# Later gate sums and a later recurrence in the second block's mixer: one core of a Trainium2

## The chip, the cores and the metric

One Trainium2 chip, of which one core is used. The time is the device time of one launch in microseconds (us), the median of three runs. A profiled execution of the same kernel gives the trace that is read below.

## What is computed

The reference is a block with retention, dilated attention and a memory cross-attention, followed by a second block of two layers. Each layer of the second block is a feed-forward network, a mixer, and another feed-forward network; the change touches the mixer alone. It has three branches over 512 positions, whose outputs are normalised one by one, joined, scaled, and projected:

```python
proj = h @ w_in
(lru_x, lru_g, sb_q, sb_k, sb_v, fx_q, fx_k, fx_v, fx_f) = jnp.split(proj, SPLIT_POINTS, axis=-1)
u = _causal_depthwise_conv(lru_x, conv_w, conv_b)
y_lru = _rg_lru(u, w_rgate, b_rgate, w_igate, b_igate, lru_lambda) * jax.nn.gelu(lru_g)
y_sb = _stick_breaking_attention(...)            # four heads, softplus and a running sum per row
log_f = jax.nn.log_sigmoid(fx_f + b_fgate)       # forget gates: their running sum is a bias of the scores
y_fox = _forgetting_attention(fq, fk, ..., log_f)
y = jnp.concatenate([_rms(y_lru), _rms(y_sb), _rms(y_fox)], axis=-1) * g_mix_out
return y @ w_out
```

## The kernel before, in words

All large products run on TensorE (PE) as three products of rounded parts (`mm3`, lines 346 to 348): a weight of 128x1024 is loaded by a DMA on SyncE's queue (SP), rounded by ScalarE (ACT) to `wh`, and the rest `wl` is taken by VectorE (DVE) or GpSimd (POOL). There are three buffers for raw weights and six for each rounded part, so weights come some steps ahead of use.

The order of TensorE's work is written out by a small planner, the class `Flow`: a main generator issues the dense products, and streams (generators that were spawned) issue the attention tiles, norms and the recurrence. Each `yield` tells the planner a cost of TensorE in its own clock, and `Wait(us)` tells it that a stream may not go on before so much planned time. A stream that is due always goes before the next `mm3` of the main generator. TensorE then runs in exactly that order, whatever the real times are. The other engines are ordered at build time by a scheduler that follows dependencies and the order in which the program traced the instructions; each engine then runs its own list in order.

`mixer2(l, ...)` runs once per layer, at about 1279 to 1545 us (layer 0) and 2303 to 2570 us (layer 1) of the span. Its stages, as the main generator goes:

- The last dense product gives the queries and keys of the stick-breaking attention and `fT`, the forget gates' raw values (line 1347).
- A token product (`dense_tok`, tile `mmt`) gives the values `v`, and another one the queries and keys of the forgetting attention. Beside them run `gates()` and four tiles `stick(t)`, t = 3, 2, 1, 0 (512 to 128 columns). A stick tile issues scores, then softplus, a scan and exponentials on ACT, DVE and POOL, waits until `v[t]` has been issued, turns the weights (tile `tp`) and multiplies them with `v` (tile `SO`). Tile t-1 begins when tile t has its softplus behind it by the planner's clock.
- `gates()` was spawned with 1.0 us of delay. It turns `fT` (tile `f`, line 1395), issues the log-sigmoid as some twenty small operations of DVE (`neg_log_sigmoid`, tiles `lp_p` and `ls_r`), waits `gate_f` = 6.0 planned us, asks for the running sums on TensorE (tile `cs`, line 1409), copies them to `NF`, and spreads them over the partitions in four tiles `fb` (line 1418), which the forgetting tiles need.
- The last dense product of eight chunks of eight `mm3` (24 matmuls each) gives the inputs of the recurrence: chunks 0 to 3 the convolution's inputs `LX`, 4 to 7 the gates `LG`. Beside it run the forgetting tiles `fox(t)`, t = 3 to 0, each closed by `finish(o, t, 2)`: squares on ACT (`fsq`), an inverse root of ten small DVE operations (`rs_m` to `rs_y`), the scaled tile `fy`, a planned wait of 4.91 us, and a turn on TensorE (`tp`<-`fy`).
- Also beside it runs the recurrence `lru`. It polls every 0.5 planned us until `opened["last"]` is set, which `fox(0)` did when the scores of its last head were issued. It then loads two gate weights `bd` (256 KB each) by SP, and issues for each of four parts two gate products (tile `lg`, line 1287), their `Tanh` (kept behind the last `Exp` of `fox(0)` on ACT by `issue_after`), and then exponentials, squares on POOL, square roots, products on POOL and scans on DVE. The gelu, the product, the squares and their sum on POOL (`acc`) need `LG` of chunk 7 for the last part.
- When all attention tiles are turned, a product of four weights with the attention outputs follows (`slab4`, tile `sl`, 96 matmuls). The recurrence's own output goes through a second product (tile `slh`), which begins with the column sums of `acc` (tile `ms`, line 464) and their inverse root (tile `bc`).

Of the kernel before, what the change touches and what calls it, by code (L numbers as in the profile page):

```python
# [13 lines left out]
AF = mybir.ActivationFunctionType  # L14
# [171 lines left out]
def _pe(n, passes=4):  # L186

    return passes * max(n, 64) / 2400.0
# [5 lines left out]
         post1=4.2, dil_tail=1.5, dil_end=5.0, dil_turn=2.3, rsqrt=3.51, norm=0.6, post=0.38,  # L194
         apart=8.0, squares=4.73, rope=10.0, rope_k=6.24, ret=4.0, ret_e=2.0, ret_gn=8.0, aq=4.0,
         ak=4.0, dil=2.0, mem=8.0, dil_1=0.11, dil_2=0.5, mem_e=6.32, mem_p=2.24, mem_q=1.5,
         lru_tanh=2.88, lru_sum=25.0, lru_end=2.52, fqk=8.0, gate_f=6.0, gate_s=0.6, finish=4.91,
         fox_1=0.9, fox_2=0.41, stick_2=0.8, stick_h=2.0, stick_o=0.0, stick_l=4.0, stick_m=1.0,
         stick=1.81, first0=10.5, first1=15.9)

# [82 lines left out]
class Core:  # L283
# [985 lines left out]
    def lru(self, l, LX, LG, HL, opened):  # L1269


        nc, I, flow = self.nc, self.I, self.flow
        while "last" not in opened:
            yield Wait(0.5)
        bd = [self.act("bd") for _ in range(2)]
        for q in range(2):
            nc.sync.dma_start(bd[q], I["m_bd"][l][:, q * 512:q * 512 + 512])
        a4, hb = self.a4[l], self.hb[l]
        U, R, G = [], [], []
        for m in range(4):  # L1280
            while len(LX) <= m:
                yield Wait(0.5)
            u = LX[m]
            r, g = self.act("lr"), self.act("li")
            for q, o in enumerate((r, g)):
                ps = self.ps("x", "lg")
                nc.tensor.matmul(ps, bd[q][:, m * 128:m * 128 + 128], u,
                                 start=True, stop=True)

                with self.tc.issue_after(opened["last"]):  # L1290
                    nc.scalar.activation(o, ps, AF.Tanh, scale=0.5,
                                         bias=hb[:, q * 4 + m:q * 4 + m + 1])
                yield _pe(512)
            nc.vector.scalar_tensor_tensor(u, g, 1.0, u, op0=OP.add, op1=OP.mult)

            nc.scalar.activation(g, r, AF.Tanh, scale=a4[:, m:m + 1], bias=a4[:, m:m + 1])
            U.append(u), R.append(r), G.append(g)
        bd.clear()
        for m in range(4):
            c = a4[:, 4 + m:5 + m]  # L1300
            nc.scalar.activation(R[m], R[m], AF.Exp, scale=c, bias=c)
        for m in range(4):
            u, a, g = U[m], R[m], G[m]

            q = self.rot("a2")
            nc.gpsimd.tensor_tensor(q, a, a, op=OP.mult)
            nc.vector.scalar_tensor_tensor(g, q, 1.0, g, op0=OP.add, op1=OP.mult)
        for m in range(4):
            u, a, g = U[m], R[m], G[m]
            nc.scalar.activation(g, g, AF.Sqrt, scale=0.25)  # L1310
            nc.gpsimd.tensor_tensor(u, u, g, op=OP.mult)

            nc.vector.tensor_tensor_scan(g, a, u, 0.0, op0=OP.mult, op1=OP.add)
        while len(LG) < 4:
            yield Wait(0.5)
        sums = []
        for m in range(4):
            nc.scalar.activation(LG[m], LG[m], AF.Gelu_apprx_tanh)
            nc.vector.tensor_tensor(U[m], G[m], LG[m], op=OP.mult)
            self.square_sum(sums, U[m], self.rot)  # L1320
        HL += [(self.act("lh", F32R), self.act("ll", F32R)) for _ in range(4)]

        def norm(hf):
            sl, out = slice(hf * 256, hf * 256 + 256), []
            yield from self.spread([sums[0][:, sl]], 2, 1.0 / 512, out)
            for m in range(4):
                t = self.half("ln")
                nc.vector.scalar_tensor_tensor(t, U[m][:, sl], self.vec(f"g_mix{l}", m), out[0],
                                               op0=OP.mult, op1=OP.mult)
                hi, lo = HL[m][0][:, sl], HL[m][1][:, sl]  # L1330
                nc.scalar.activation(hi, t, AF.Copy)
                nc.vector.tensor_tensor(lo, t, hi.bitcast(F32), op=OP.subtract)
        yield Wait(T["lru_sum"])
        yield from norm(0)
        opened["half"] = flow.t
        yield from norm(1)

    def mixer2(self, l, H, H2):
# [53 lines left out]
        def gates():  # L1392
# [22 lines left out]
            for h in range(4):  # L1415
# [6 lines left out]
                nc.scalar.activation(o, ps, AF.Copy)  # L1422
                FB.append(o)
                yield 4 * _pe(128)
        gated = flow.spawn(gates(), 1.0)

        YT = {}

# [28 lines left out]
        def finish(o, t, y0):  # L1457
# [3 lines left out]
            rs = self.rsqrt(ss, 1, 1.0 / 256, RMS_EPS)  # L1461
            y = self.half("fy")
            nc.vector.tensor_scalar(y, o, rs, None, op0=OP.mult)
            yield Wait(T["finish"])
            ps = self.flip([y[:, p * 128:p * 128 + 128] for p in range(2)])
            sl = slice(t * 128, t * 128 + 128)
# [7 lines left out]
        def fox(t):  # L1474
# [10 lines left out]
            def score(h):  # L1485
                if h % 2 == 0:
# [6 lines left out]
                c = slice(h, h + 1)  # L1493
                nc.vector.tensor_tensor(b[:, c], nf[:, c], m[:, c], op=OP.subtract)
                nc.vector.tensor_tensor(b[:, c], b[:, c], nf[:, c], op=OP.subtract)
                last = nc.scalar.activation(e[:, :n], e[:, :n], AF.Exp, bias=b[:, c],
                                            accum_out=lsum[:, c])
                if (t, h) == (0, 3):
                    opened["last"] = last.ins
                return 0.0 if h % 2 else _pe(n) + 0.2  # L1500

            def second(h):
# [57 lines left out]
        opened = {}  # L1560
# [128 lines left out]
```

## Time and profile before

| | |
|---|---|
| median of 3 runs | 2929.01 us (2927.82 to 2929.83) |
| profiled execution, device time | 2929.86 us |
| its span, first to last instruction | 2928.1 us |
| TensorE busy | 2783.2 us of the span, mean granted clock 0.974 |
| VectorE, ScalarE, GpSimd busy | 1540.9, 1033.7, 382.2 us |

The views are read in this order: the busy share of each engine, TensorE's waits by what ended them, the timelines around the two longest kinds of wait, and the busy times and granted clock of the stretches there. Times in timelines are us from the span's start; a number in square brackets is the idle time of that engine just before, and behind it stands what ended it.

### The profile page before, as it was taken

What the parts mean: (1) busy time and instruction counts of PE and PEld (TensorE: products, weight loads), DVE (VectorE), ACT (ScalarE), POOL (GpSimd) and SP (SyncE); (2) the same over time, 40 slices, a digit from 0 to 9 for tenths busy, and PEclk for the clock granted to TensorE, in tenths of its full rate; (3) what the DMA queues carried; (4) which work ended last, traced back from release to release, by engine and by line L of the source; (5) the groups of instructions that cost most, each with busy time, mean ns of one, the idle gap of its engine ahead of it and who ended that gap; (6) DMA issues with size and microseconds to landing.
All of it is one profiled execution on the core that took longest, in us unless ns stands there. A gap on an engine that the chain in (4) does not pass through costs nothing.

```text
span 2928.1 us, 36992 instructions
## 1 busy us (share of the span) xinstructions
PE 2783.2 (95%) x14492; PEld 2360.2 (81%) x14492; DVE 1540.9 (53%) x2973; ACT 1033.7 (35%) x1739; POOL 382.2 (13%) x376
## 2 busy tenths in 40 slices
PE   8999998999989999979889999999999898899999
PEld 7888878888878888877678888888888775788888
DVE  6465656645455444457666454464334576643333
ACT  4355443323233222345534222342223455342221
POOL 3010304101041000131221000110001312210000
PEclk9999999999989999989989999999999899899999
DMA  4322332645524555311115555354322121232322
GB/s 162 119 75 88 93 94 65 184 159 173 161 86 137 158 173 158 113 53 65 51 59 165 158 173 158 115 166 129 101 94 92 53 65 44 59 100 87 107 87 72
DMA packets 94607, 326.07 MB, mean 111 GB/s; under 512 B 11232, under 2 KB 15584, under 8 KB 94432
## 3 DMA queue, kind: packets, MB, share of 16 engines
q1 hardware_dynamic: 94288, 323.53, 35.4%
q8 instruction: 114, 1.87, 0.3%
q14 instruction: 61, 0.50, 0.1%
q10 hardware_dynamic: 144, 0.18, 0.0%
HBM read 321.37 MB, written 2.10 MB: 110 GB/s over the span
## 4 chain that ended last, share of the span: by engine, by line
PE 84%; DVE 10%; ACT 3%; POOL 2%; issue 1%; DMA 1%; POOLq 0%; ACTq 0%; DVEq 0%
PE mm L346 15%; PE mm L348 15%; PE mm L347 15%; PE dn L348 6%; PE dn L346 6%; PE dn L347 6%; PE mmt L346 2%; PE mmt L347 2%; PE mmt L348 2%; PE slh L347 2%; PE slh L346 2%; PE slh L348 2%; PE tp L684 1%; DVE wl L340 1%; PE sl L347 1%
## 5 line engine op out<-in xcount | busy, mean ns | idle before, releaser
L338 ACT ACTIVATE wh<-wr 128x1024 fp32r<-128x1024 f32 x456 | 481.9, 1059 | 1266.0 <-PE mm L347 504.4
L346 PE MATMUL mm<-hh,wh 128*128 128x512 f32 (+1 forms) x2344 | 862.1, 368 | 4.8 <-ACT hh L527 1.9
L347 PE MATMUL mm<-hl,wh 128*128 128x512 f32 (+1 forms) x2344 | 855.0, 365 | 2.5 <-DVE hl L500 2.4
L348 PE MATMUL mm<-hh,wl 128*128 128x512 f32 (+1 forms) x2344 | 854.3, 364 | 3.0 <-DVE wl L340 3.0
L340 DVE TENSOR_TENSOR wl<-wr,wh 128x1024 fp32r<-128x1024 f32 x440 | 542.6, 1236 | 326.4 <-ACT wh L338 324.9
L346 PEld LDWEIGHTS mm<-hh,wh 128*128 128x128 f32 x2344 | 450.1, 192 | 73.5 <-ACT hh L527 2.2
L348 PEld LDWEIGHTS mm<-hh,wl 128*128 128x128 f32 x2344 | 449.3, 192 | 71.3 <-DVE wl L340 3.6
L347 PEld LDWEIGHTS mm<-hl,wh 128*128 128x128 f32 x2344 | 449.9, 192 | 69.8 <-DVE hl L500 3.2
L795 DVE CUSTOM_DVE_ANT_0 ada<-ada,c 128x1024 f32<-128x1024 f32 x144 | 179.1, 1244 | 317.8 <-DMA ada<-in_w_ada_dram 317.8
L348 PE MATMUL dn<-uh,wl 128*128 128x512 f32 x720 | 280.5, 390 | 0.0
L347 PE MATMUL dn<-ul,wh 128*128 128x512 f32 x720 | 280.5, 390 | 0.0
L346 PE MATMUL dn<-uh,wh 128*128 128x512 f32 x720 | 280.5, 390 | 0.0
L490 POOL TENSOR_TENSOR acc<-sq,sq 128x256 f32<-128x256 f32 (+1 forms) x34 | 38.5, 1133 | 1330.7 <-ACT sq L487 1330.7
L633 DVE TENSOR_TENSOR sg<-mm,sg 128x512 f32<-128x512 f32 x110 | 75.8, 690 | 183.5 <-PE mm L348 179.2
L347 PEld LDWEIGHTS dn<-ul,wh 128*128 128x128 f32 x720 | 135.2, 188 | 28.0
L348 PEld LDWEIGHTS dn<-uh,wl 128*128 128x128 f32 x720 | 135.2, 188 | 28.0
L346 PEld LDWEIGHTS dn<-uh,wh 128*128 128x128 f32 x720 | 135.2, 188 | 27.9
L346 PE MATMUL mmt<-wh,hh 128*128 128x512 f32 x352 | 145.4, 413 | 10.5 <-ACT wh L338 8.0
L347 PE MATMUL mmt<-wl,hh 128*128 128x512 f32 x352 | 140.1, 398 | 0.5 <-DVE wl L340 0.5
L348 PE MATMUL mmt<-wh,hl 128*128 128x512 f32 x352 | 139.8, 397 | 0.0
L490 POOL TENSOR_TENSOR acc<-acc,sq 128x256 f32<-128x256 f32 (+1 forms) x140 | 122.3, 874 | 83.4 <-ACT sq L487 45.0
L669 DVE SCALAR_TENSOR_TENSOR X<-dn,gate,X 128x512 f32<-128x512 f32 x64 | 48.0, 750 | 153.7 <-PE dn L348 153.7
(324 smaller groups left out, 3627.6 us busy)
## 6 DMA issues: line engine op xcount, KB each, us to landing
wr<-in_f_gu_dram SPq DMA_DIRECT2D x176, 512.0 KB, 3.5
ada<-in_w_ada_dram SPq DMA_DIRECT2D x144, 512.0 KB, 4.2
wr<-in_f_dn_dram SPq DMA_DIRECT2D x88, 512.0 KB, 3.5
wr<-in_w_gu_dram SPq DMA_DIRECT2D x44, 512.0 KB, 3.6
wr<-in_w_in_dram SPq DMA_DIRECT2D x28, 512.0 KB, 3.6
wr<-in_m_t_dram SPq DMA_DIRECT2D x24, 512.0 KB, 3.5
wr<-in_w_dn_dram SPq DMA_DIRECT2D x22, 512.0 KB, 3.7
wr<-in_m_v_dram SPq DMA_DIRECT2D x16, 512.0 KB, 3.6
```

Of the source, the lines that this page charges most:

```text
L338: nc.scalar.activation(hi, raw, AF.Copy)
L340: (e or nc.vector).tensor_tensor(lo, raw, hi.bitcast(F32), op=OP.subtract)
L346: mm(ps, ah, bh, start=start, stop=False)
L347: mm(ps, ah, bl, start=False, stop=False)
L348: mm(ps, al, bh, start=False, stop=stop)
L490: nc.gpsimd.tensor_tensor(acc, accs.pop(), sq, op=OP.add)
L633: nc.vector.tensor_tensor(t, ps, t, op=OP.mult)
L669: self.nc.vector.scalar_tensor_tensor(self.X[m], ps, gate(m), self.X[m], op0=OP.mult, op1=OP.add)
L684: self.nc.tensor.transpose(ps[:, j * 128:j * 128 + 128], b, self.ident)
L795: nc.vector.tensor_tensor_reduce(out=w, in0=w, in1=c, scale=1.0, scalar=0.0, op0=OP.mult, op1=OP.add, accum_out=ml[:, i:i + 1])
```

## The change

The wait of `gates()` between the log-sigmoid and the sums grows from 6 to 24 planned us and the stream starts 4.0 instead of 1.0 us after its spawn. `opened["last"]` is now set by `finish` of the last forgetting tile, behind the tracing of its norm; the recurrence polls every 0.3 instead of 0.5 us. The order constraint of `Tanh` behind the last `Exp` goes. After each gate product the stream waits 0.3 planned us, so that one `mm3` of the main generator comes between two products.

```diff
-         lru_tanh=2.88, lru_sum=25.0, lru_end=2.52, fqk=8.0, gate_f=6.0, gate_s=0.6, finish=4.91,
+         lru_tanh=2.88, lru_sum=25.0, lru_end=2.52, fqk=8.0, gate_f=24.0, gate_s=0.6, finish=4.91,
...
         while "last" not in opened:
-            yield Wait(0.5)
+            yield Wait(0.3)
...
-                with self.tc.issue_after(opened["last"]):
-                    nc.scalar.activation(o, ps, AF.Tanh, scale=0.5,
-                                         bias=hb[:, q * 4 + m:q * 4 + m + 1])
+                nc.scalar.activation(o, ps, AF.Tanh, scale=0.5,
+                                     bias=hb[:, q * 4 + m:q * 4 + m + 1])
                 yield _pe(512)
+                yield Wait(0.3)
...
-        gated = flow.spawn(gates(), 1.0)
+        gated = flow.spawn(gates(), 4.0)
...
             nc.vector.tensor_scalar(y, o, rs, None, op0=OP.mult)
+            if (t, y0) == (0, 2):
+
+                opened["last"] = True
             yield Wait(T["finish"])
...
-                last = nc.scalar.activation(e[:, :n], e[:, :n], AF.Exp, bias=b[:, c],
-                                            accum_out=lsum[:, c])
-                if (t, h) == (0, 3):
-                    opened["last"] = last.ins
+                nc.scalar.activation(e[:, :n], e[:, :n], AF.Exp, bias=b[:, c],
+                                     accum_out=lsum[:, c])
```

## Rows read from the trace of the kernel before

**Rows 1.** Part 1 of the page: engines, busy us, share, instructions.
```profile
PE 2783.2 (95%) x14492; PEld 2360.2 (81%) x14492; DVE 1540.9 (53%) x2973; ACT 1033.7 (35%) x1739; POOL 382.2 (13%) x376
```

**Rows 2.** Waits of PE, whole span: engine, line, waited for; us, times, longest.
```profile
PE tp L684 <- DVE fy L1463: 36.4, 4, 16.7
...
PE cs L1409 <- DVE ls_r L1246: 23.7, 2, 12.7
...
PE f L1395 <- ACT fT L1347: 2.9, 2, 1.5
```

**Rows 3.** Timeline (start, us, engine, line, tiles), forget gates of layer 0.
```profile
1302.37 0.18 DVE L1246 TENSOR_TENSOR ls_r<-ls_r,lp_p 128x16 f32<-128x16 f32 x1
...
1302.70 0.56 PE L1409 MATMUL cs<-ls_r,tri 128*128 128x4 f32 x2 [12.74 <-DVE ls_r L1246]
...
1308.38 4.73 PE L1418 MATMUL fb<-ident,NF 128*128 128x128 f32 x32
```

**Rows 4.** Stretches: length, PE, PEld, DVE, ACT, POOL busy, granted clock, DMA, GB/s.
```profile
1289.00:1303.00 14.00, 1.26 (x7) 0.79 (x5) 13.38 (x23) 6.39 (x12) 6.49 (x4) 0.66 0.02 6
1303.00:1308.00 5.00, 5.00 (x23) 4.81 (x23) 0.17 (x1) 0.00 (x0) 0.00 (x0) 0.50 0.00 0
```

**Rows 5.** The same columns, the stretch of the stick tiles behind the sums.
```profile
1303.00:1345.00 42.00, 40.00 (x234) 33.76 (x233) 17.38 (x30) 17.66 (x34) 5.72 (x4) 0.91 0.15 51
```

**Rows 6.** Timeline, stick tile t = 2 of layer 0, and the turns that use it.
```profile
1315.15 0.92 PE L1437 MATMUL S<-sqk,sqk 64*128 64x384 f32 x4
...
1323.82 0.53 ACT L1541 ACTIVATE z<-z 128x384 f32<-128x384 f32 x1 [1.39 <-POOL z L1540]
...
1330.84 0.53 ACT L1541 ACTIVATE z<-z 128x384 f32<-128x384 f32 x1 [1.43 <-POOL z L1540]
...
1332.19 1.69 PE L684 MATMUL tp<-ident,z 128*128 128x128 f32 x14
```

**Rows 7.** Timeline, last two forgetting tiles and gate products; last row is layer 1.
```profile
1439.03 0.40 ACT L1460 ACTIVATE fsq<-fo 128x256 f32<-128x256 f32 x1
...
1440.35 1.13 PE L1287 MATMUL lg<-lx,bd 128*128 128x512 f32 x2
...
1444.44 0.35 DVE L1463 TENSOR_SCALAR fy<-fo,rs_y 128x256 f32<-128x256 f32 x1
...
1446.50 4.51 PE L1287 MATMUL lg<-lx,bd 128*128 128x512 f32 x10
...
1460.27 0.40 ACT L1460 ACTIVATE fsq<-fo 128x256 f32<-128x256 f32 x1
...
1471.83 1.43 DVE L1463 TENSOR_SCALAR fy<-fo,rs_y 128x256 f32<-128x256 f32 x1
...
1473.41 0.66 PE L684 MATMUL tp<-ident,fy 128*128 128x128 f32 x2 [16.73 <-DVE fy L1463]
...
2496.30 0.66 PE L684 MATMUL tp<-ident,fy 128*128 128x128 f32 x2 [16.41 <-DVE fy L1463]
```

**Rows 8.** Stretches (columns of rows 4): cold restart behind the turn, and the attention product.
```profile
1473.00:1478.00 5.00, 4.59 (x13) 3.71 (x14) 2.10 (x4) 0.73 (x2) 0.12 (x1) 0.53 0.31 105
...
1482.00:1502.00 20.00, 20.00 (x89) 16.54 (x89) 10.80 (x13) 4.53 (x6) 1.30 (x1) 1.00 0.30 91
```

**Rows 9.** Timeline, end of the recurrence: its sums on POOL and their use.
```profile
1471.85 1.26 POOL L490 TENSOR_TENSOR acc<-acc,sq 128x512 f32<-128x512 f32 x1
...
1484.84 1.30 POOL L490 TENSOR_TENSOR acc<-acc,sq 128x512 f32<-128x512 f32 x1 [11.72 <-issue]
...
1502.91 0.50 PE L464 MATMUL ms<-ones,acc 128*128 128x1 f32 x4
```

**Rows 10.** Timeline of SP's queue: the gate weights, and the weight loads behind them.
```profile
1430.27 0.90 SPq L1277 DMA_DIRECT2D bd<-in_m_bd_dram  x2
1443.48 31.27 SPq L336 DMA_DIRECT2D wr<-in_m_o_dram  x2
```

**Rows 11.** Stretch (columns of rows 4): forgetting tiles between chunks of the dense product.
```profile
1380.00:1425.00 45.00, 42.60 (x250) 32.78 (x251) 32.12 (x97) 15.63 (x37) 5.83 (x3) 1.00 0.20 59
```

## Prediction

> **What bounds the kernel now.** I read the page first: TensorE is busy for 95% of the span, no other engine for much over half [rows 1]. So a gain can only come from the time in which TensorE stands still or runs at its lower clock, and that is read from its waits. Three of them are in the second block's mixer, once for each layer [rows 2]: turns of `fy` (36.4 us, nearly all of it in two long waits), the sums `cs` behind the log-sigmoid (23.7 us in two), and the turn of `fT` (2.9 us in two). The timelines then say why.
>
> The sums: TensorE comes to `cs` with nothing left to do before it and waits 12.74 us for `ls_r` [rows 3]. In that stretch VectorE is busy for 13.38 of 14 us [rows 4]: the twenty small operations of the log-sigmoid go between the wide ones of stick tile 3. The order asks for the sums too early; other products (`mmt`) stand behind them in TensorE's list and could have run.
>
> The turn of `fy`: the norm of the last forgetting tile begins with its squares on ScalarE at 1460.27, with no idle time of ScalarE ahead of it, 9.3 us after the last gate product ended (1446.50 plus 4.51): its list held the recurrence's functions first. The scaling on VectorE follows at 1471.83, behind the scans, and TensorE waits 16.73 us in layer 0 and 16.41 us in layer 1 [rows 7]. The tile before, whose norm had no recurrence ahead of it, needed 5.8 us from its squares to its `fy` (1439.03 to 1444.79) [rows 7]. Behind each long wait TensorE goes on at its lower level of 1.2 GHz: granted 0.50 and 0.53 in the two stretches that follow [rows 4, 8], against 1.00 in the next product [rows 8].
>
> **Part by part: the sums.** `fT`'s turn moves behind the scores of stick tile 3, by when `fT` is long written: the 2.9 us go, and nothing waits for `f` but the log-sigmoid. The sums move 24 planned us behind that. The first token product is 32 `mm3` of 0.64 planned us, so with the scores of two tiles (2 x 1.05 and 2 x 0.84) it ends at about 24.5 planned us, and the sums stand at about 28.2, among the turns of stick tiles 3 and 2. That is some 20 us of TensorE's work later than now, against a wait of 12.7, so the wait goes: 12.7 and 11.0 us (23.7 less 12.7). The forgetting tiles, which use `fb`, begin only behind the second token product, so nobody misses it. With the wait the restart at 1.2 GHz goes. A stretch of 5 us at 0.50 [rows 4] holds at most 2.5 us of that; with what follows I bound it by 0 and 4 and take 2 per layer, near the row.
>
> What is late next is VectorE. It has the same work, and TensorE is now ahead of it. The turns of stick tiles 3 and 2 stand at 1332.19 [rows 6]. Take off the 12.74, the 1.4 of `fT`, and the sums with `fb`, which now come later (1302.70 to 1313.1 [rows 3] less one `mm3`, 9.1 us), and some 1.5 of clock: they would come at about 1307.5. VectorE is full until 1302.4. Tile 2 needed 9.2 us from its scores to its second head's weights (1315.15 to 1324.35) and 16.2 us to its fourth [rows 6]; if it only gets VectorE at 1302.4, the second head is there at 1311.6, 4 us late. With about 1 us for a copy of `v` or `NF` in ScalarE's or VectorE's list I take 5 us per layer of new waits. Bounds: 0 (tile 2's copies and softplus fit between) and all of 12.7 (VectorE stays the end of the chain). Against the upper one speaks the stretch behind, where VectorE is busy for 17.38 of 42 us [rows 5]: it can catch up. Layer 0: 1.4 + 12.7 + 2 - 5 = 11.1; layer 1: 1.5 + 11.0 + 2 - 5 = 9.5. Together 20.6 us.
>
> **The recurrence.** It now starts when the norm of the last tile has been traced, so squares, root and `fy` stand ahead of it in all lists, and the removed constraint on `Tanh` costs nothing: the products it reads come behind the last tile on TensorE anyway. The two `bd` loads go 10 us later in the program. Now they are issued at 1430.27, ten us before the first product [rows 7, 10]. If SP takes them behind the load at 1443.48 [rows 10], they still land about when the first product stands (1448); behind the second load of that row they would hold TensorE for some us. I take 0, bounds 0 and 8.
>
> TensorE's work is only reordered. At 1440.35 two of eight chunks (16 `mm3`) are left. About seven fill the waits of the last tile where gate products stand now, and the rest alternate with the eight products, which cost 0.90 us each now (five in 4.51 us [rows 7]). The turn of `fy` stands 4.91 planned us behind the norm's tracing, which itself comes 1.09 planned us behind the last product with `v`; that is 6 us and more against the 5.8 measured for the tile before [rows 7], so I leave 0.5 us, bounds 0 and 3. The waits of 16.73 and 16.41 us go. The restart goes too: 13 matmuls took 5 us, and at the rate of the product (89 in 20 us, 0.225 each) they take 2.9 [rows 8]: 2.1 us per layer. Changing between gate products and `mm3` eight times may cost 0.1 us each, 1 us in all with the other engine-side gaps, bounds 0 and 2.
>
> Late next is the recurrence itself. From the last gate product's end (1451.0) to the sum of its third part (1473.1) it took 22.1 us; the fourth sum waited for chunk 7 and adds its own 1.3 us [rows 7, 9], so 23.4 us. In the new order the last product and the last chunk end together, and then the attention product covers 96 x 0.225 = 21.6 us until `ms` asks for the sum (today it asks 16.8 us after it: 1486.14 to 1502.91 [rows 9]). So 2 us of wait per layer; bounds 0 (the first three parts run ahead in the spaced products) and 12 (VectorE's 10.80 us of evacuations and weight parts in 20 us of that product [rows 8] stand ahead of the scans). Per layer: 0.5 + 1 + 2 = 3.5 us of new cost. Sum: 16.73 + 16.41 + 2 x 2.1 - 2 x 3.5 = 30.3 us.
>
> Both parts: 50.9 us. The profiled execution took 2929.86 us, its span 2928.1; minus 50.9 is 2879.0. It lies 0.85 above the median of the runs, so **2878 us**.
>
> **Rivals.** (A) *The stick tiles take the place of the sums' wait*: VectorE's list, not the order, is the end, and only `fT`'s 2.9 us stay of the first part: 2929 - 30.3 - 2.9 = 2896. For it: 13.38 of 14 us busy [rows 4]; against it: its idle time right behind [rows 5]. (B) *The recurrence becomes the wait*: `ms` waits 12 us instead of 2, or `bd` lands 8 us late; some 9 us more per layer: 2897. For it: 23.4 against 21.6 us leaves no slack; against it: three of four parts start earlier against the last product than now. (C) *Slower, by the clock*: the lower level is kept where TensorE alternates between short pieces and then into the attention product. A busy TensorE does run at 0.50 for five us behind a wait [rows 4]. At 0.385 us per matmul (5 us by 13 [rows 8]) instead of 0.225 the 16 + 32 `mm3` cost 144 x 0.16 = 23 us more and the gate products 7 more, 30 per layer: 2878 + 60 = 2938. It decides only if about 85% of that stretch is at 1.2 GHz. Against it: the forgetting tiles between chunks, an equally mixed stretch, have 1.00 throughout [rows 11].
>
> The Trainium skill's page "TensorE: Matmul & The Clock Gate" (section "A second HAM failure mode: psum-queue depth-cycling") speaks for C: short idle times between groups of matmuls can make the clock swing between its levels. By that rule the time would be 2938; the trace's 1.00 in the mixed stretch does not bear it out, so it keeps a small chance.
>
> (D) *It does not do what it says*: ScalarE's list still has the recurrence's functions ahead of the squares, and only the first part counts: 2929 - 20.6 = 2908.
>
> **How the numbers follow.** A measurement of this kernel tells 0.2% (5.9 us) from no change. Forecast, 2864 to 2892: 0.58. No new wait at all (17 us better, 2861): 0.05. A: 0.14. B: 0.10. A and B (2915): 0.03. D: 0.03. A and D together (2926, no change): 0.03. C: 0.04. The range from 2864 to 2903 holds the forecast, A and B, 0.82. Faster 0.93, same 0.03, slower 0.04.
>
> **What would show it.** Right: `tp`<-`fy` under 5 us in all and `cs`<-`ls_r` gone among TensorE's waits; `fsq` of the last tile within 2 us of its input; granted clock near 1 from 1290 to 1345 and from 1440 to the end of the attention product; new, small waits of `tp` for stick weights and of `ms` for `acc`. Wrong: a wait at `tp`<-`z` of over 8 us per layer (A), at `ms`<-`acc` or `lg`<-`bd` of over 8 us (B), a granted clock near 0.5 in the attention product (C), or `fy` still late (D).

## The result, and the profile after

The changed kernel takes 2896.63 us, the median of four runs (2888.67 to 2897.36), against 2929.14 us for the kernel before beside it: a ratio of 0.9883, 95% interval 0.9866 to 0.9901. The profiled execution took 2897.36 us, 32.5 less than the one before. The forecast was 2878: the direction is right, the gain of 51 us is too large by 18. The time lies inside the stated range (2864 to 2903), but in the part of it that was held for rivals A and B, not in the forecast's own 2864 to 2892.

The longest waits of TensorE over the whole span in the profile after, and below them the same two in the profile before (us in total, times, longest). They answer to [rows 2].

```profile
PE bc L476 <- DVE rs_y L453: 33.6, 17, 8.1
PE mmt L346 <- ACT v L1566: 17.8, 4, 6.5
```

```profile
PE bc L476 <- DVE rs_y L453: 24.9, 17, 4.6
...
PE mmt L346 <- ACT v L1566: 2.5, 2, 1.2
```

All three waits of [rows 2] are gone from the head of the list: `fy`, `cs` behind `ls_r`, and `f`. The two above have grown. In the mixer of layer 0 (1270 to 1560 us) they are 9.4 us for `rs_y` and 9.2 us for `v`. A value product (`mmt`) waits for ScalarE's copy of an earlier value (`v`), which gives its buffer in PSUM back (PSUM holds what TensorE's products write); the first `bc` waits for the root of the recurrence's norm (`rs_y`). The timelines of the first one, on TensorE, ScalarE, VectorE and POOL in turn (start, duration, engine, line, operation, idle time before and its end):

```profile
1302.86 0.79 PE L346 MATMUL mmt<-wh,hh 128*128 128x512 f32 x1 [6.51 <-ACT v L1566]
...
1319.84 0.50 PE L346 MATMUL mmt<-wh,hh 128*128 128x512 f32 x1 [2.69 <-ACT v L1566]
...
1301.69 0.63 ACT L1541 ACTIVATE z<-z 128x512 f32<-128x512 f32 x1 [1.12 <-POOL z L1540]
1302.22 0.58 ACT L1566 ACTIVATE v<-mmt 128x512 f32<-128x512 f32 x1
...
1296.44 1.21 DVE L1538 TENSOR_TENSOR_SCAN ab<-ones,ab 128x512 f32<-128x512 f32 x1
1297.58 0.14 DVE L1233 TENSOR_TENSOR lp_p<-lp_p,lp_q 128x16 f32<-128x16 f32 x1
...
1298.78 1.16 DVE L1234 TENSOR_SCALAR lp_p<-lp_p 128x16 f32<-128x16 f32 x1
...
1300.46 1.23 DVE L1233 TENSOR_TENSOR lp_p<-lp_p,lp_q 128x16 f32<-128x16 f32 x1
...
1302.92 1.28 DVE L1233 TENSOR_TENSOR lp_p<-lp_p,lp_q 128x16 f32<-128x16 f32 x1
...
1297.73 3.92 POOL L1540 TENSOR_TENSOR z<-z,ab 128x512 f32<-128x512 f32 x2 [1.92 <-DVE lp_p L1233]
1302.90 1.27 POOL L1540 TENSOR_TENSOR z<-z,ab 128x512 f32<-128x512 f32 x1 [1.25 <-DVE lp_p L1234]
```

Read it backwards: `mmt` starts at 1302.86 when the copy of `v` ends; the copy stands in ScalarE's list behind an exponential of stick tile 3, which waited for two of POOL's products `z`. These began at 1297.73, behind a scan on VectorE (`ab`) and a small operation of the log-sigmoid (`lp_p`), to which the profile puts the wait down; between the scans stand more of these operations, some of them over 1 us long. It is the same VectorE list that `cs` used to wait for [rows 3]; the wait only came to TensorE through another name.

The granted clock behind the first wait and behind the second, and then in the recurrence's part (windows of the profile after; length, busy time and count of PE, PEld, DVE, ACT and POOL, then TensorE's clock, DMA share and GB/s):

```profile
1303.00:1312.00 9.00, 9.00 (x30) 7.22 (x31) 7.29 (x14) 6.69 (x15) 2.52 (x3) 0.74 0.01 2
...
1320.00:1340.00 20.00, 20.00 (x117) 19.52 (x118) 3.72 (x6) 5.64 (x11) 0.00 (x0) 0.66 0.24 80
...
1436.00:1461.00 25.00, 23.85 (x107) 16.24 (x106) 11.89 (x54) 20.30 (x39) 3.44 (x2) 1.00 0.13 43
1461.00:1484.00 23.00, 22.36 (x98) 17.82 (x96) 19.94 (x21) 19.62 (x24) 14.16 (x10) 1.00 0.00 0
```

In the recurrence's part the last tile's norm now goes ahead, as asked for, and TensorE runs at 1.00 from 1436 to 1484. The rows that answer to [rows 7] and [rows 9], from ScalarE, VectorE and TensorE, then VectorE's list ahead of the root:

```profile
1446.97 0.42 ACT L1459 ACTIVATE fsq<-fo 128x256 f32<-128x256 f32 x1 [0.58 <-DVE fo L1511]
...
1449.39 0.35 DVE L1462 TENSOR_SCALAR fy<-fo,rs_y 128x256 f32<-128x256 f32 x1
...
1453.97 0.38 PE L684 MATMUL tp<-ident,fy 128*128 128x128 f32 x2
...
1484.65 0.61 PE L464 MATMUL ms<-ones,acc 128*128 128x1 f32 x4 [0.93 <-POOL acc L490]
1493.33 1.20 PE L476 MATMUL bc<-ident,rs_y 128*128 128x128 f32 x4 [8.07 <-DVE rs_y L453]
...
1488.06 0.14 DVE L447 TENSOR_SCALAR rs_m<-ms 128x2 f32<-128x2 f32 x1
1488.18 1.22 DVE L340 TENSOR_TENSOR wl<-wr,wh 128x1024 fp32r<-128x1024 f32 x1
...
1490.97 1.22 DVE L340 TENSOR_TENSOR wl<-wr,wh 128x1024 fp32r<-128x1024 f32 x1 [1.09 <-ACT wh L338]
```

The same `bc` in the profile before:

```profile
1506.89 1.22 PE L476 MATMUL bc<-ident,rs_y 128*128 128x128 f32 x4 [3.48 <-DVE rs_y L453]
```

The sum is there at 1485.3, but VectorE takes it up at 1488.06, behind weight parts (`wl`) and updates of `X`, and stops for two more parts between the root's small operations.

To see where the time went I cut each layer's mixer at four points of TensorE's timeline: the first value product, the first softmax score (`S`<-`fT`), the first attention product (`sl`) and the first product of the recurrence's projection (`slh`). Stage 1 lies between the first two, the softmax heads and recurrence between the next, the attention product and the recurrence's norm between the last. Microseconds, layer 0 / layer 1, for all kernels of this study:

| kernel | stage 1 | heads | product and norm | median us | ratio to before, 95% |
|---|---|---|---|---|---|
| before | 109.2 / 109.4 | 92.8 / 92.6 | 28.0 / 28.0 | 2929.14 to 2930.79 | |
| after | 107.6 / 105.1 | 73.6 / 72.4 | 34.5 / 33.9 | 2896.63 | 0.9866 to 0.9901 |
| gates_only | 103.4 / 105.1 | 97.6 / 94.1 | 28.0 / 28.0 | 2924.01 | 0.9968 to 0.9987 |
| recur_only | 109.4 / 109.5 | 73.3 / 70.7 | 34.1 / 33.9 | 2899.51 | 0.9883 to 0.9910 |
| spare_buffer | 107.3 / 107.6 | 73.8 / 72.4 | 34.2 / 33.8 | 2896.93 | 0.9874 to 0.9901 |
| late_logsig | 101.9 / 99.8 | 73.3 / 70.8 | 33.8 / 34.2 | 2883.03 | 0.9823 to 0.9850 |
| late_and_spare | 101.7 / 108.3 | 73.4 / 72.3 | 34.2 / 34.0 | 2897.28 | 0.9880 to 0.9913 |
| no_spacing | 107.6 / 105.2 | 73.6 / 72.3 | 43.2 / 42.3 | 2908.20 | 0.9917 to 0.9942 |
| few_tables | 103.5 / 105.0 | 74.6 / 73.0 | 34.7 / 34.8 | 2892.64 | 0.9860 to 0.9887 |
| both_late | 102.9 / 102.8 | 73.5 / 71.4 | 34.2 / 33.9 | 2883.17 | 0.9828 to 0.9855 |
| parts_on_pool | 104.8 / 104.2 | 73.6 / 72.3 | 36.7 / 36.7 | 2896.76 | 0.9872 to 0.9902 |
| early_root | 101.7 / 104.9 | 73.3 / 72.3 | 38.2 / 35.5 | 2894.30 | 0.9865 to 0.9894 |
| all_three | 101.8 / 99.8 | 73.6 / 71.4 | 32.0 / 30.2 | 2880.65 | 0.9813 to 0.9845 |
| later_logsig | 96.6 / 93.6 | 77.5 / 73.8 | 29.8 / 29.7 | 2871.15 | 0.9781 to 0.9809 |

The rows of before and after give the balance: stage 1 gained 1.6 and 4.3 us, the heads 19.2 and 20.2, the product and norm lost 6.5 and 5.9. Sum: 5.9 + 39.4 - 12.4 = 32.9 us, against 32.5 between the two profiled executions.

Two cautions belong to this table. Its stage times are from one profiled execution each, its medians from all runs. And a stage's time holds TensorE's clock as well as its waits: after, gates_only, no_spacing, few_tables, parts_on_pool and early_root have the same list of operations in stage 1 on TensorE, VectorE, ScalarE and POOL alike, and it takes them 101.7 to 107.6 us in layer 0. In early_root and the last two rows work has also moved across a cut, as is said there.

### The profile page after: what moved, and what is told of

The parts are those of the page before. It is cut to its first block, busy times and chain, and to the rows that moved or that the text cites. A ratio compares the mean times of both kernels' runs of the same rounds, so it can differ in the third digit from the quotient of the medians.

```text
span 2895.5 us, 37017 instructions
## 1 busy us (share of the span) xinstructions
PE 2782.0 (96%) x14492; PEld 2358.3 (81%) x14492; DVE 1536.1 (53%) x2973; ACT 1055.9 (36%) x1755; POOL 383.5 (13%) x376
## 3 DMA queue, kind: packets, MB, share of 16 engines
q1 hardware_dynamic: 94288, 323.53, 36.1%
## 4 chain that ended last, share of the span: by engine, by line
PE 82%; DVE 10%; ACT 4%; POOL 2%; issue 1%; DMA 1%; POOLq 0%; ACTq 0%; DVEq 0%
PE mm L346 15%; PE mm L348 15%; PE mm L347 15%; PE dn L347 6%; PE dn L346 6%; PE dn L348 6%; PE mmt L346 2%; PE mmt L347 2%; PE mmt L348 2%; PE slh L347 2%; PE slh L346 2%; PE slh L348 2%; DVE wl L340 2%; PE tp L684 1%; DVE rs_a L452 1%
## 5 line engine op out<-in xcount | busy, mean ns | idle before, releaser
L347 PEld LDWEIGHTS mm<-hl,wh 128*128 128x128 f32 x2344 | 448.6, 191 | 72.3 <-issue 3.6
L348 PEld LDWEIGHTS mm<-hh,wl 128*128 128x128 f32 x2344 | 448.0, 191 | 71.4 <-DVE wl L340 3.6
```

Of the source, the lines that this page charges most:

```text
L347: mm(ps, ah, bl, start=False, stop=False)
L348: mm(ps, al, bh, start=False, stop=stop)
```

## Experiments

### Each part alone

gates_only is the kernel before with the gates' edit, recur_only the kernel after without it. The diffs from here on show only what changes in a line where the line is long; `...` stands for code left out.

```diff
# gates_only, against before
-gate_f=6.0
+gate_f=24.0
...
-gated = flow.spawn(gates(), 1.0)
+gated = flow.spawn(gates(), 4.0)
# recur_only, against after
-gate_f=24.0
+gate_f=6.0
...
-gated = flow.spawn(gates(), 4.0)
+gated = flow.spawn(gates(), 1.0)
```

gates_only:

> The kernel before with the first part alone: gate_f 24 and the gates' process begun 4 planned us in; the recurrence is as in before. Theory (a queue behind VectorE takes the place of the sums' wait): in the profile after, the first value product of the second half waits 6.5 us in layer 0 and 6.4 us in layer 1 for the ScalarE copy of a value that gives its PSUM buffer back, and from the layer's first value product to the first softmax score the layers gained 1.6 and 4.2 us; so this kernel is 2 to 6 us under before, 2923 to 2927. Rival (the forecast's own term, with something else taking the gain back between the two): 16 to 21 us under before, 2908 to 2913, and no value product that waits over 2 us for that copy.

recur_only:

> The kernel after with the gates as they were (gate_f 6, begun 1 planned us in): the recurrence's part alone. Theory (the two parts are independent, and the recurrence's own gain is 19.1 and 20.3 us up to the end of the attention product, less 6.6 and 6.0 in the projection behind it): 26 to 28 us under before, 2901 to 2903. Rival (the parts lean on each other, the later gates taking ScalarE or VectorE time that the recurrence then has or lacks): under 20 or over 32 us.

Measured: gates_only 2924.01 us, 5.8 under before (2929.8); recur_only 2899.51, 30.3 under it. So the recurrence's part is worth what the forecast gave it (30.3), a little more than the 26 to 28 I had written before the run, and the gates' part is worth 5.8 instead of 20.6. The two add up to 36.1 us where the changed kernel gained 32.5; with the recurrence's part in place the gates add 2.9 us between medians. Each part shows its own waits alone. TensorE's waits in layer 0 of gates_only:

```profile
PE tp L684 <- DVE fy L1463: 16.4, 1, 16.4
PE mmt L346 <- ACT v L1566: 9.0, 2, 6.3
```

and of recur_only:

```profile
PE cs L1408 <- DVE ls_r L1246: 11.0, 1, 11.0
PE bc L476 <- DVE rs_y L453: 9.1, 3, 7.7
```

The wait for `v` belongs to the gates, that for the root to the recurrence. gates_only's heads are longer than before's by 4.8 and 1.5 us, with no more idle time (22.9 against 23.1 us in layer 0), but with a lower granted clock there: 0.92 from 1388 to 1430 where before has 1.00. What made it lower I did not find.

### Stage 1: the copy's place, or the chain behind it?

spare_buffer lets the second value pair take a PSUM buffer of the other pool, so that it needn't wait for the copy; late_logsig takes the log-sigmoid out of the way of stick tile 3 (the sums then stand 32 planned us behind `fT`'s turn instead of 24); late_and_spare does both.

```diff
# spare_buffer
-pss = [self.ps("x" if t0 and first else "mm", "mmt") for _ in range(2)]
+pss = [self.ps("x" if t0 and (first or e and i) else "mm", "mmt") for i in range(2)]
# late_logsig
-gate_f=24.0
+gate_f=14.0
...
+yield 0.2
+yield Wait(18.0)
 nlf = self.neg_log_sigmoid(fy, 16)
-yield 0.2
 yield Wait(T["gate_f"])
```

spare_buffer:

> The kernel after, with one thing changed where the value products run: the second pair of tiles takes one of its two PSUM buffers from the other pool, so that its first product needn't wait for the ScalarE copy of the value before it. Theory (the place of that copy in ScalarE's list, behind a stick exponential, is what PE waits for): the waits of 6.5 and 2.7 us per layer fall to under 3 in sum, the kernel is 6 to 14 us under after, 2883 to 2891. Rival (the stick tiles' chain on VectorE and POOL is the limit and the copy only stands in it): the same idle time comes back at a transpose of a stick weight, waiting for z, and the time is within 3 us of after.

late_logsig:

> The kernel after with the forget gates' log-sigmoid itself asked for 18 planned us later, beside the sums and no longer ahead of them among the first stick tiles' work. Theory (the log-sigmoid's VectorE operations, up to 1.3 us each, stand ahead of the stick tiles' there, and the value's copy stands on ScalarE behind the stick exponential that waits for them): the value product's wait of 6.5 us falls to 1 to 4, the kernel is 4 to 10 us under after, 2887 to 2893. Rival (the stick tiles' own chain is as long without it): the wait only gets another name, a stick weight's transpose waiting for z, and the time is within 2 us of after.

late_and_spare:

> The later log-sigmoid and the spare PSUM buffer together. Theory (in late_logsig the two waits for the copy of a value, 3.9 and 5.4 us in layer 0, are the stick tiles' chain again, as in spare_buffer): the wait gets the name of a stick transpose or of the product with its weights, time within 2 us of late_logsig, 2881 to 2885. Rival (with the log-sigmoid gone from there the copy is the limit): 4 to 9 us under late_logsig, 2874 to 2879.

Measured: spare_buffer 2896.93 us, no different from after. My theory of the copy's place fell; the rival held. The waits of layer 0 in spare_buffer:

```profile
PE SO L1452 <- ACT pT L326: 6.5, 2, 6.3
PE tp L684 <- ACT z L1541: 3.5, 2, 2.2
```

10.0 us instead of 9.2, now at the stick tiles' own products. The copy was the messenger; the stick tiles' chain through VectorE, POOL and ScalarE is the limit.

late_logsig took 2883.03 us, 13.6 under after and more than I had expected. Its two waits in layer 0:

```profile
1299.79 0.50 PE L346 MATMUL mmt<-wh,hh 128*128 128x512 f32 x1 [3.85 <-ACT v L1567]
...
1318.83 0.80 PE L346 MATMUL mmt<-wh,hh 128*128 128x512 f32 x1 [5.37 <-ACT v L1567]
```

Here the theory's mechanism held only in part: the first wait fell by 2.7 us, the second grew by 2.7, since the small operations now stand between the copies and scans of stick tile 2 (VectorE has them from 1300.2 to 1309.2). Their sum stayed at 9.2 us. The later place of the sums has no part in this: they stand behind both waits in either kernel (1325.9 in after, 1335.7 here). The stage gained 5.7 and 5.3 us all the same: the sum of all idle times before TensorE's rows in the stage fell from 13.6 to 10.9 us in layer 0 and from 13.3 to 10.2 in layer 1, and the rest is clock. So 5.8 of the 13.6 us are idle time that went; that the rest follows from the edit is not shown.

late_and_spare shows the clock's part by itself. It took 2897.28 us, 14 more than late_logsig, and neither of my two expectations for it was right. In layer 0 its stage 1 is as short as late_logsig's (101.7 against 101.9); in layer 1 it is 8.5 us longer. A window of layer 1 in late_and_spare:

```profile
2315.00:2343.00 28.00, 21.45 (x92) 18.36 (x93) 14.81 (x30) 11.91 (x25) 3.43 (x2) 0.50 0.24 75
```

and in late_logsig:

```profile
2315.00:2343.00 28.00, 22.63 (x167) 20.18 (x166) 18.58 (x45) 14.78 (x33) 5.92 (x6) 0.94 0.24 76
```

TensorE is busy for about the same time in both, but does 92 matmuls at 0.50 in one and 167 at 0.94 in the other. In late_and_spare the longest wait in it is one of 6.3 us (`SO` behind `pT`), in late_logsig none is longer than 4.5 us in that stage. The length of the wait doesn't explain the clock: in layer 0 of late_and_spare the same wait is 7.2 us, and the same stretch has more clock, not less:

```profile
1312.00:1340.00 28.00, 19.73 (x129) 17.81 (x129) 16.78 (x37) 13.56 (x31) 5.04 (x4) 0.76 0.24 76
```

It is not one odd execution either: the mean granted clock of late_and_spare's four runs is 0.973 to 0.978, of late_logsig's 0.981 to 0.985.

### The recurrence: spacing, table loads, VectorE's list

no_spacing takes the 0.3 planned us between gate products away.

```diff
# no_spacing
 yield _pe(512)
-yield Wait(0.3)
```

no_spacing:

> The kernel after without the 0.3 planned us between the gate products of the recurrence. Theory (TensorE's order of these ten products among the last attention tile's work sets nothing, since ScalarE's list is what the recurrence waits for): within 3 us of after, 2894 to 2900. Rival (unspaced products take the PSUM buffers ahead of the scores, and attention waits for the Tanhs that give them back): 4 to 12 us over after, with a score or a transpose that waits over 2 us for a Tanh.

Measured: 2908.20 us, 11.6 over after. My theory that the spacing sets nothing fell, and the rival named the wrong victim. Waits of layer 0:

```profile
PE sl L347 <- DVE yl L500: 7.7, 2, 6.1
PE bc L476 <- DVE rs_y L453: 4.9, 3, 3.5
PE sl L346 <- ACT yh L499: 2.9, 1, 2.9
```

The attention product waits for the last tile's two halves, `yh` on ScalarE and `yl` on VectorE: unspaced, the recurrence's functions stand in a block ahead of them in those lists. That costs 10.6 us, and the root's wait, which is short here, gives 4.5 back. The stretch is 8.7 and 8.4 us longer (43.2 and 42.3 against 34.5 and 33.9), 4.7 and 5.5 of it idle time; the rest goes with a lower granted clock, 0.78 against 0.90 in layer 0. So about two fifths of the recurrence's gain (11.6 of 27 to 30 us) hang on a number whose worth I had put at nothing in this expectation.

few_tables puts ScalarE's square roots behind its last exponential and its Gelus behind the last root; both_late adds late_logsig.

```diff
# few_tables
-nc.scalar.activation(R[m], R[m], AF.Exp, scale=c, bias=c)
+ex = nc.scalar.activation(R[m], R[m], AF.Exp, scale=c, bias=c)
...
-nc.scalar.activation(g, g, AF.Sqrt, scale=0.25)
+with self.tc.issue_after(ex.ins):
+    sq = nc.scalar.activation(g, g, AF.Sqrt, scale=0.25)
...
-nc.scalar.activation(LG[m], LG[m], AF.Gelu_apprx_tanh)
+with self.tc.issue_after(sq.ins):
+    nc.scalar.activation(LG[m], LG[m], AF.Gelu_apprx_tanh)
```

few_tables:

> The kernel after with ScalarE's recurrence in an order with few table loads: the square roots of all four blocks behind the last exponential, the Gelus behind the last square root (3 loads in that stretch instead of 10, at 1.28 us each). Theory (ScalarE's loads hold up the weights' first halves, with them VectorE's weight parts and the X copies, and with them the root that the next projection's first product waits 8.1 us for): the wait of the first bc for rs_y falls towards the 3.5 us of before, and the kernel is 8 to 11 us under after (4 to 5.5 per layer), 2886 to 2889. Rival (VectorE's list ahead of the root is too long whatever ScalarE does): the wait stays over 7 us and the time within 2 us of after. Second rival (roots in a bunch come later for the scan, and acc with them): a wait of ms for acc of over 4 us, no gain or a loss.

both_late:

> The few table loads and the later log-sigmoid in one kernel. Theory (two stages with limits of their own): the gains add, 2896.6 less 4.0 less 13.6, 2877 to 2882. Rival (what few_tables measured was the clock of the first stage, which one execution of after itself had, not its own stage): no lower than late_logsig alone, 2881 to 2885.

The first expectation came from ScalarE's rows in the profile after, where an `ACT_TABLE_LOAD` stands at each change of function, ten of them between 1439 and 1477:

```profile
1467.18 1.28 ACT L1309 ACT_TABLE_LOAD   x1
1468.48 0.63 ACT L1309 ACTIVATE li<-li 128x512 f32<-128x512 f32 x1
1469.13 1.28 ACT L1300 ACT_TABLE_LOAD   x1
```

Measured: few_tables 2892.64 us and both_late 2883.17, the first 4.0 under after, between what theory and rival gave, the second no different from late_logsig, as its rival had it. The root's wait did fall to 3.48 us, and its place was taken at once:

```profile
1475.57 0.79 PE L346 MATMUL sl<-yh,wh 128*128 128x512 f32 x1 [4.09 <-DVE X L1597]
```

The scans now come in one block of four (7.75 us) and the updates of `X` wait behind it. Heads, product and norm together are 109.3 and 107.8 us against 108.1 and 106.3 of after: nothing was gained there. The profiled execution is 0.9 us under after's: stage 1 is 4.1 us shorter in layer 0 (103.5 against 107.6), where few_tables changed nothing, and the rest is longer. The 4.0 us between the medians can't be divided from these profiles. The loads did not set when the recurrence is done: its sum is ready 22.5 us behind the first attention product instead of 23.5. Nine table loads less per layer (3 instead of the 12 that after has from 1432 to 1477; 9 x 1.28 = 11.5 us of ScalarE) were worth nothing by themselves.

parts_on_pool makes the second halves (`wl`) of the weights of the recurrence's own product (`slh`) on POOL; early_root asks for the recurrence's norm 11 planned us sooner.

```diff
# parts_on_pool
-ws += [self.weights(srcs[i]) for i in range(4)]
+ws += [self.weights(srcs[i], e) for i in range(4)]
... # with e = nc.gpsimd handed down from the mixer
# early_root
-lru_sum=25.0
+lru_sum=14.0
```

parts_on_pool:

> The kernel after with the second halves of the projection's four weights made on POOL instead of VectorE. Theory (VectorE's backlog ahead of the root is the end of that stage: four parts of 1.2 us stand in it): the wait of the first bc for rs_y falls from 8.1 to 3.5 to 5 us, the kernel is 6 to 9 us under after, 2888 to 2891. Rival (POOL, which adds up the squares in the same stretch, is late with acc or with the parts instead): a wait of ms for acc or of a projection product for wl of over 2 us, and the time within 2 us of after or above it.

early_root:

> The kernel after with the recurrence's norm asked for 14 planned us after its squares instead of 25, so that its root stands ahead of the weight parts and the last X updates in VectorE's list. Theory (the root waits in VectorE's list behind parts whose weights come late; moving the parts to POOL left two others in front of it): the first bc's wait for rs_y falls from 8.1 to under 4, and the kernel is 3 to 9 us under after, 2888 to 2894. Rival (the sum of squares is done no sooner, and its product, now ahead of the last of the attention products in PE's list, holds them up): a wait of ms for acc of 5 us or more takes its place, and the time is within 2 us of after or above it.

Measured: 2896.76 and 2894.30 us, neither apart from after by more than its runs spread. Both rivals' waits came (2.3 us of `ms` for `acc` in parts_on_pool, 7.7 in early_root), and parts_on_pool's time with them; early_root's, 2.3 us under after, lies between its two expectations. In parts_on_pool the root's wait grew to 9.0 us: VectorE begins the root at once and then stops in the middle of it:

```profile
1481.67 0.16 DVE L447 TENSOR_SCALAR rs_m<-ms 128x2 f32<-128x2 f32 x1 [2.16 <-PE ms L464]
1484.37 2.29 DVE L340 TENSOR_TENSOR wl<-wr,wh 128x1024 fp32r<-128x1024 f32 x1 [2.54 <-ACT wh L338]
1486.58 0.15 DVE L448 TENSOR_SCALAR rs_y<-rs_m 128x2 int32<-128x2 int32 x1
1487.88 1.23 DVE L340 TENSOR_TENSOR wl<-wr,wh 128x1024 fp32r<-128x1024 f32 x1 [1.14 <-ACT wh L338]
```

Two parts of the next block's weights stand between the root's small operations, and their ScalarE halves are not there yet. Moving work off VectorE did not shorten this wait, which comes from what VectorE itself waits for in its list. early_root puts the root ahead of those parts, and the wait goes to the sum (TensorE's rows):

```profile
1478.04 0.37 PE L464 MATMUL ms<-ones,acc 128*128 128x1 f32 x1 [7.67 <-POOL acc L490]
...
1488.06 0.35 PE L476 MATMUL bc<-ident,rs_y 128*128 128x128 f32 x1 [1.97 <-DVE rs_y L453]
```

The sum is ready 23.4 us behind the first attention product, as in after (23.5), so asking for it sooner only hands the wait on. What sets that time is not traced further; the table loads account for 1.0 us of it, as few_tables shows, and no_spacing, with its gate products in a block, has the sum at 19.4. In this kernel, and in the two below, another `bc` waits 1.7 us for its root behind the first `slh` products, which is behind the table's last cut; after has no such wait.

### Taking the ends off together

all_three is late_logsig with few_tables and early_root; later_logsig is the same with `Wait(42.0)` in place of `Wait(18.0)` ahead of the log-sigmoid.

all_three:

> The later log-sigmoid, the few table loads and the earlier root together. Theory (each table load less brings acc forward by what the earlier root can then use): 4 to 8 us under late_logsig, 2875 to 2879. Rival (X updates, scans and roots share VectorE, and the order alone frees nothing): 2881 to 2886, like both_late.

later_logsig:

> The three of all_three, with the log-sigmoid asked for 42 planned us later instead of 18, so that all its VectorE operations stand behind the stick tiles' scans that the value products wait for. Theory (VectorE's share in the stick tiles' chain is the first stage's limit, and each operation taken out of it shows in the wait for the value's copy): the two waits, 9.0 us in layer 0 in all_three, fall to 4 to 6, and the kernel is 4 to 12 us under all_three, 2869 to 2877. Rival (the chain is bound by ScalarE's exponentials and POOL's products, and the 21 small operations fill gaps): both waits stay within 1 us, 2878 to 2883. Second rival (the gates come too late for the softmax heads): a wait of the gates' sums or of a bias of over 4 us at the heads' scores, and 2883 or more.

Measured: all_three 2880.65 us, 2.4 under late_logsig, between what its two theories gave (its runs lie from 2873 to 2885). In its profile heads, product and norm are 105.6 and 101.6 us against late_logsig's 107.1 and 105.0: 4.9 us together, where neither edit alone gave any. But most of that is lost again behind the last cut: from there to the next layer's mixer all_three takes 1.7 us longer, and from the second layer's cut to the end 2.0 us longer, with this wait in it:

```profile
1491.40 1.22 PE L476 MATMUL bc<-ident,rs_y 128*128 128x128 f32 x4 [1.72 <-DVE rs_y L453]
```

The profiled executions differ by 1.3 us, and the runs of the two kernels overlap, so a gain from the two edits together is not shown. later_logsig took 2871.15 us, 9.5 under all_three, within the theory's range. Its waits in layer 0:

```profile
PE mmt L346 <- ACT v L1569: 6.8, 2, 3.5
PE sl L346 <- DVE X L1598: 3.6, 1, 3.6
...
PE bc L476 <- DVE rs_y L453: 3.1, 3, 1.7
```

With all of the log-sigmoid behind the stick tiles' scans, the wait for `v` falls from 9.0 to 6.8 us (no longer than 3.5 at once). The expectation put it at 4 to 6, so its time came true with less of its mechanism. Stage 1 is 96.6 and 93.6 us, but that is not a gain of this size: 27 of its matmuls (nine `mm3` of the last dense product) now stand behind its end, and its idle time rose from 10.5 us in both layers to 11.8 and 12.0, with waits of `tp` for `fy` and of `SO` for `pT`. Stage 1 and heads together are 1.3 and 3.8 us shorter than in all_three, the product and norm 2.1 and 0.5. No wait of the heads is over 4 us. This is the fastest kernel of the study: 0.9795 of before (0.9781 to 0.9809), below the changed kernel.

## Why the prediction was right in direction and wrong in size

**What it got right.** The three long waits went as forecast, and for the reasons given: `fsq` follows its input directly, and the turn of the last tile's `fy` has no wait. The `bd` loads cost nothing. The sum of the recurrence is late by 0.9 us, against 2. The restart at 1.2 GHz went with the `fy` wait: TensorE's rows between the first score and the first attention product add up to 69.7 us of busy time before and 67.6 in recur_only in layer 0 (stage less idle time), 2.1 as forecast; in layer 1 it is 70.4 and 65.8, 4.6 less, so the size came true in one layer of two. The whole part measured 30.3 us alone, the forecast figure; in the balance of the profile after it is 39.4 - 12.4 = 27.0.

Within that figure two errors cancel nearly, so the agreement to a tenth is luck. Forecast was 3.5 us per layer of new cost, and there was 6 at the end of the stretch, mostly a root 4.6 us later than before (a wait of 8.07 us against 3.48). I had priced the sum's lateness and not what stands in VectorE's list between the sum and the root. The heads, on the other side, gained 19.2 and 20.2 us, 2 to 3 more than the wait and the restart less 1.5 of new cost.

**The step that failed** is stage 1's term for what is late next: "I take 5 us per layer of new waits", and beside it the 2 us of clock that were to come back. The old waits that went are 14.1 and 12.5 us. The stage's idle time (18.7 and 17.1 us before, 13.6 and 13.3 after) fell by 5.1 and 3.8 only, so the new waits are 9.0 and 8.7 us in the two layers: inside my bounds (0 to 12.7), nearly twice the value taken. I priced only the second head's weights (4 us late) and 1 us for copies; but the copy of `v` stands behind the third exponential of tile 3 in ScalarE's list, and so the value product took over the whole chain's lateness. The argument against the upper bound, VectorE's idle time in the stretch behind [rows 5], counted for nothing, since the chain waits ahead of that stretch.

The clock's 2 us did not come back in the profile after. Stage 1's busy time in layer 0 is 109.2 - 18.7 = 90.5 us before and 107.6 - 13.6 = 94.0 after: 3.5 more, where 2 less was forecast. In layer 1 it is 0.5 less. Of the 14.7 us that stage 1 fell short of its 20.6, this is 7.0, the waits 7.7. But the waits are the steady half: the five other kernels with after's lists in stage 1 have 13.4 to 13.9 us of idle time there in layer 0, and 87.8 (early_root) to 94.1 us (no_spacing) of busy time, so the clock's half differs from kernel to kernel and its sign is open. The forecast "granted clock near 1 from 1290 to 1345" is wrong: 0.74 and 0.66 in two of its windows. In this profile one long wait with one restart [rows 4] became two shorter ones with two.

**The rivals.** A's time (2896) is the measured one, and its mechanism, VectorE and the stick tiles in place of the sums' wait, is what spare_buffer shows; but its sign did not show, since the wait is named after `v` and not after `z`, and its sum was another: 5.9 and 27.0 us, not 2.9 and 30.3, so that the totals meet is in part chance. B had the right place for the other 4.6 us per layer and the wrong end of it: behind `ms`, not ahead of it. C fell: 1.00 in both windows from 1436 to 1484, as the mixed stretch of before had it, and 2938 was not the time. The Trainium skill's page "TensorE: Matmul & The Clock Gate" (section "A second HAM failure mode: psum-queue depth-cycling") tells of a kernel whose clock swings between its levels because TensorE stands idle for short times between groups of matmuls; these rows don't show that for this stretch. D fell with `fsq` at 1446.97.

## What to carry to other kernels

When an order is changed so that a wait on a busy engine's chain goes, price the next user of that same chain on every list it runs through, the copy that gives back a buffer too: a wait that gets another name is not a gain. Take out of the chain what isn't needed there (here the log-sigmoid's 22 small operations: moving only the products that use them gave 5.8 us, moving the operations too 13.6 more in late_logsig, of which 5.8 are idle time and the rest goes with the clock), and expect that when one end of a chain is shortened another takes its place. And do not count on clock coming back from one long wait when shorter waits take its place. When a stage table shows a gain, see first whether the work between its cuts is the same.

## What the hardware showed that I had not expected

**A small VectorE operation can take as long as the POOL product beside it.** The operation of line 1233 on 128x16 elements takes 0.18 us at 1291.35, with POOL idle:

```profile
1291.35 0.18 DVE L1233 TENSOR_TENSOR lp_p<-lp_p,lp_q 128x16 f32<-128x16 f32 x1
```

From 1302.92 it takes 1.28 us, where POOL's product of 128x512 runs from 1302.90 for 1.27 us: both end at 1304.2. The Trainium skill's page "SBUF — State Buffer" (section "SBUF: two separate sides") says that a VectorE operation with two inputs in SBUF (against a POOL operation that reads SBUF), or one in a mode that uses two ports, and a POOL operation share a pair of ports, and that whichever starts first holds it for its whole length; the two rows agree. The pattern has no exception among the 56 operations of lines 1233 and 1234 in the profile after: the 8 that overlap a POOL instruction take 1.16 to 1.28 us, the other 48 0.14 to 0.18. Line 1234 has one input tile and is stretched as well (1.16 us from 1298.78); whether it runs in such a mode no row shows. The kernel before has four of them in the stretch of [rows 4], 5.05 us in all. By this reading, part of VectorE's 13.38 busy us there, from which the forecast took it to be full, was waiting for POOL.

**The clock can differ where the instructions don't.** In after and in early_root stage 1 has the same operations in the same order, and up to 1320 us nearly the same rows. Behind the second wait they part. Windows of early_root, which answer to those of after in the first section:

```profile
1303.00:1312.00 9.00, 9.00 (x32) 7.14 (x31) 7.29 (x14) 6.68 (x15) 2.52 (x3) 0.75 0.01 2
...
1320.00:1340.00 20.00, 19.01 (x156) 17.32 (x155) 8.99 (x27) 9.12 (x22) 0.20 (x1) 1.00 0.26 76
```

Between the two windows both have 1.00 and 28 matmuls. After has 0.66 and 117 matmuls in the last window, early_root 1.00 and 156, and its stage is 5.9 us shorter. Runs of one kernel spread by about as much (2888.67 to 2897.36 for after), so a difference of 4 us between these kernels, as few_tables first seemed to give, has to be looked for in the stage that was edited. What decides between the two levels after such a wait stays open.
